# Stores moved to GpSimd's DMA queue in a WKV recurrence kernel

## The chip, the cores and the metric

The kernel runs on one core of one Trainium2 chip. The metric is device time in microseconds (us) of one execution, the median of several; the profile is of one execution and shows a span that is a little shorter than the timed one. The engines of the core are PE (TensorE, matmuls), DVE (VectorE), ACT (ScalarE), POOL (GpSimd) and SP (SyncE, which here only issues DMAs). DMAs can be issued by SP, ACT and POOL.

## The reference

For each of 16 batches and 256 channels a recurrence runs over 2048 time steps. It keeps a weighted sum `aa` of values and a sum `bb` of weights, with a running maximum `pp` so that no exponential overflows:

```python
for t in range(seq_len):
    ww = u + k[b, t]
    qq = np.maximum(pp, ww)
    e1, e2 = np.exp(pp - qq), np.exp(ww - qq)
    output[b, t] = (e1 * aa + e2 * v[b, t]) / (e1 * bb + e2 + 1e-08)
    ww = pp - w + k[b, t]
    qq = np.maximum(ww, k[b, t])
    e1, e2 = np.exp(ww - qq), np.exp(k[b, t] - qq)
    aa, bb, pp = e1 * aa + e2 * v[b, t], e1 * bb + e2, qq
```

k, v and the output are float32 arrays of 16 x 2048 x 256, 33.55 MB each, so 67.1 MB are read and 33.55 MB written.

## The kernel before

The kernel cuts time into 16 chunks of 128 steps, and each chunk into 4 groups of four batches. One such piece of k, v or the output is 128 x 1024 float32 values, 0.524 MB, and is called a pair; there are 64 of them, n = 4c + p for chunk c. The main loop has one slot for each pair. In slot n the exponentials of pair n are made (`exps`), k of pair n+2 is rounded for the matmuls (`round_k`), v of pair n+1 is cast to bfloat16 (`cast_v`), and the output of pair n-11 is finished: `den` and `recip` of pair q = n-10 make the reciprocals of its denominators in a buffer `rd`, and `num` and `mult` of pair qp = n-11 multiply the numerators in. Between them, spread over some slots, stand the steps that carry the state from chunk to chunk (`state_...`, `turn`, `inject`); `inject` writes the state into the ring EZR with four small DMAs, before `den` of the chunk's first pair reads it.

All large transfers go through SP's queue, in program order; only some loads of v, which convert to bfloat16 as they go, and the small transfers of `inject` are issued by GpSimd:

```python
    kpool = ctx.enter_context(tc.tile_pool(name="kpool", bufs=AHEAD))     # AHEAD = 6
    vpool = ctx.enter_context(tc.tile_pool(name="vpool", bufs=5))
    vbpool = ctx.enter_context(tc.tile_pool(name="vbpool", bufs=4))
    rpool = ctx.enter_context(tc.tile_pool(name="rpool", bufs=6))
# ... cut ...
    def v_mode(n):
        return "dma" if n >= LAG and n % 4 == 3 else "dve"                # LAG = 10
# ... cut ...
    def load_v(n, queue=SP):
        if v_mode(n) == "dma":
            VB[n] = vbpool.tile([128, 4, Dm], BF16, tag="vb", name="vb")
            K(POOL.dma_start(out=VB[n], in_=rows_of(v, n)))
        else:
            vr_of[n] = vpool.tile([128, 4, Dm], F32, tag="vr", name="vr")
            K(queue.dma_start(out=vr_of[n], in_=rows_of(v, n)))

    def load(n):
        for x, f in ((n - 1, load_v), (n, load_k)) if n < LAG + AHEAD else ((n, load_k), (n, load_v)):
            if x < NP and (f == load_k or v_mode(x) != "dma"):
                f(x)
# ... cut ...
    def state_next(c):
        # ... the state of the next chunk, two small operations on POOL ...
        if 4 * c + 11 < NP:
            load_v(4 * c + 11)
# ... cut ...
    def store(n):
        K(SP.dma_start(out=rows_of(out, n), in_=RD.pop(n).rearrange("p i (n d) -> p (i n) d", n=2)))
```

The main loop from slot 10 on, with the state steps (`small_work`) left in:

```python
    for n in range(LAG, NP):
        q, qp = n - LAG, n - LAG - 1
        load(n + AHEAD)
        if qp >= 0:
            num(qp, NUMB, 0)
        den(q)
        small_work(n, "nums")
        exps(n)
        small_work(n, "act")
        if qp >= 0:
            mult(qp, NUMB, 0)
        small_work(n, "mid")
        if n + 2 < NP:
            round_k(n + 2)
        if n + 1 < NP:
            cast_v(n + 1)
        # ... cut ...
        if qp >= 0:
            num(qp, NUMB, 1)
        sums(n - 1)
        recip(q, lambda: small_work(n, "recip"))
        if qp >= 0:
            mult(qp, NUMB, 1)
        small_work(n, "scan")
        if qp >= 0:
            store(qp)
        if n + 1 < NP:
            times_v(n)
            small_work(n, "chain")
            logs(n + 1)
        # ... cut ...
```

After the last slot eleven more rounds finish the outputs that are still open.

Of the kernel before, what the change touches and what calls it, by code (L numbers as in the profile page):

```python
# [11 lines left out]
ACT = mybir.ActivationFunctionType  # L12
# [3 lines left out]
def kernel(  # L16
# [9 lines left out]
    K = tc.keep_in_program_order  # L26
    PE, DVE, SC, POOL, SP = nc.tensor, nc.vector, nc.scalar, nc.gpsimd, nc.sync
# [6 lines left out]
    NP = 4 * NST  # L34
    RING = 12
    AHEAD = 6
    LAG = 10
# [5 lines left out]
    kpool = ctx.enter_context(tc.tile_pool(name="kpool", bufs=AHEAD))  # L43
    vpool = ctx.enter_context(tc.tile_pool(name="vpool", bufs=5))
    vbpool = ctx.enter_context(tc.tile_pool(name="vbpool", bufs=4))
    rpool = ctx.enter_context(tc.tile_pool(name="rpool", bufs=6))
    small = ctx.enter_context(tc.tile_pool(name="small", bufs=2))
    tiny = ctx.enter_context(tc.tile_pool(name="tiny", bufs=1))
    ps = ctx.enter_context(tc.tile_pool(name="ps", bufs=1, space=bass.MemoryType.PSUM))
# [2 lines left out]
    kr_of, vr_of, VB = {}, {}, {}  # L52

    def v_mode(n):
        return "dma" if n >= LAG and n % 4 == 3 else "dve"

    def rows_of(x, n):
        c, p = divmod(n, 4)
        return x[4 * p:4 * p + 4, c * TC:(c + 1) * TC, :].rearrange("n t d -> t n d")

    def load_k(n, queue=SP):
        kr_of[n] = kpool.tile([128, 4, Dm], F32, tag="kr", name="kr")
        K(queue.dma_start(out=kr_of[n], in_=rows_of(k, n)))
# [8 lines that stand above are left out]


    def load(n):
        for x, f in ((n - 1, load_v), (n, load_k)) if n < LAG + AHEAD else ((n, load_k), (n, load_v)):
            if x < NP and (f == load_k or v_mode(x) != "dma"):
                f(x)

# [99 lines left out]
    def round_k(n):  # L180
        km = consts.tile([128, 4, Dm], F32R, tag=f"km{n % 2}", name="km") if n < 2 else KM[n - 2]
        K(DVE.tensor_copy(km, kr_of.pop(n)))  # L182
        KM[n] = km
# [21 lines left out]
    def exps(n):  # L205
        if n < TURNS:
            for q in range(2):
                K(SC.activation(ez(n)[:, q], half(n, q), ACT.Exp))  # L208
        else:
            K(SC.activation(ez(n)[:, 0:2], PS[:, 0:4, :].rearrange("p (q i) x -> p q i x", q=2), ACT.Exp))  # L210

    def cast_v(n):
        mode = v_mode(n)
        if mode == "dma":
            return
        vb = vbpool.tile([128, 4, Dm], BF16, tag="vb", name="vb")
        vr = vr_of.pop(n)
        if mode == "act":
            K(SC.activation(vb, vr, ACT.Copy))
        elif mode == "pool":  # L220
            K(POOL.tensor_copy(vb, vr))
        else:
            K(DVE.tensor_copy(vb, vr))  # L223
        VB[n] = vb

    def times_v(n):
        vb = VB.pop(n).rearrange("p (i n) d -> p i (n d)", i=2)
        K(DVE.tensor_mul(ez(n)[:, 2:4], ez(n)[:, 0:2], vb.unsqueeze(1).broadcast_to([128, 2, 2, D])))  # L228
# [16 lines left out]
    def sums(n):  # L245
        c, p = divmod(n, 4)
        t = MISC[:, 0:Dm]
        for o in range(2):
            x = 24 - 16 * o - 2 * p
            for j in range(4):  # L250
                q, i = divmod(j, 2)
                K(PE.matmul(t[32 * j:32 * j + 32, :], mats["OH"][:, x:x + 32],  # L252
                            ez(n)[:, 2 * q, i, Dm * o:Dm * o + Dm],
                            start=p == 0 and o == 0, stop=p == 3 and o == 1,
                            tile_position=(0, 32 * j), skip_group_check=True))
# [97 lines left out]
    RD = {}  # L353

    def den(n):
        for m, q in (("L", 0), ("Id", 1)):
            for i in range(2):
                K(PE.matmul(DENB[:, i, :], mats[m], ez(n)[:, q, i, :], start=q == 0, stop=q == 1,  # L358
                            skip_group_check=True))
# [9 lines left out]
    def num(n, bank, i):  # L369
        for m, q in (("LN", 2), ("IdN", 3)):  # L370
            K(PE.matmul(bank, mats[m], ez(n)[:, q, i, :], start=q == 2, stop=q == 3, skip_group_check=True))  # L371

    def mult(n, bank, i):
        rd = RD[n]
        K(DVE.tensor_mul(rd[:, i, :], bank, rd[:, i, :]))  # L375

    def store(n):
        K(SP.dma_start(out=rows_of(out, n), in_=RD.pop(n).rearrange("p i (n d) -> p (i n) d", n=2)))

    def last_outputs(n, H):  # L380
        c, p = divmod(n, 4)
# [7 lines left out]
    for c in range(NST):  # L389
        s = 4 * c + 3  # L390
        plan = [(s + 1, "act" if s + 1 < LAG else "recip", copy_sums), (s + 1, "pe", turn),
                (s + 2, "act", state_logs), (s + 2, "mid", state_frames), (s + 2, "scan", state_scan), (s + 2, "scan", state_offsets),
                (s + 3, "recip", state_weights), (s + 3, "chain", state_chain),
                (s + 4, "nums", turn_back), (s + 4, "mid", inject), (s + 4, "mid", state_next)]
        if c == 0:
            plan = [(s + 1, "act", copy_sums), (s + 1, "pe", turn), (s + 2, "act", state_logs),
                    (s + 2, "chain", state_frames), (s + 2, "chain", state_scan), (s + 2, "chain", state_offsets),
                    (s + 3, "act", state_weights), (s + 3, "chain", state_chain),
                    (s + 4, "logs", turn_back), (s + 4, "logs", inject), (s + 4, "round", state_next)]
        if c == 1:  # L400
            plan = [(s + 1, "act", copy_sums), (s + 1, "pe", turn), (s + 2, "act", state_logs),
                    (s + 2, "chain", state_frames), (s + 2, "chain", state_scan), (s + 2, "chain", state_offsets)] + plan[6:]
        if c == NST - 1:
            plan = [(s + 1, "copy", copy_sums), (s + 1, "turn", turn),
                    (s + 1, "post", state_logs), (s + 1, "mid", state_frames), (s + 1, "mid", state_scan), (s + 1, "mid", state_offsets),
                    (s + 2, "post", state_weights), (s + 2, "first", state_chain),
                    (s + 3, "turn", turn_back), (s + 3, "first", inject)]
        for slot, where, f in plan:
            later.setdefault((slot, where), []).append((f, c))

    def small_work(n, where):
        for f, c in later.pop((n, where), []):
            f(c)
# [10 lines left out]
    logs(0)  # L424
    round_k(1)
    cast_v(0)
    for n in range(LAG):

# [19 lines left out]
    for n in range(LAG, NP):  # L448

        q, qp = n - LAG, n - LAG - 1  # L450
        load(n + AHEAD)
        if qp >= 0:
            num(qp, NUMB, 0)
        den(q)
# [17 lines that stand above are left out]
        if qp >= 0:  # L472
            mult(qp, NUMB, 1)
        small_work(n, "scan")
        if qp >= 0:
            store(qp)
        if n + 1 < NP:
            times_v(n)
            small_work(n, "chain")
            logs(n + 1)  # L480
        else:
            den(q + 1)
        small_work(n, "pe")
    sums(NP - 1)
    small_work(NP, "copy")
    late = []
    for n in range(NP, NP + LAG + 1):

        q, qp = n - LAG, n - LAG - 1
        H = PS[:, 2 * (n % 2):2 * (n % 2) + 2, :]  # L490
        for i in range(2):
            num(qp, H[:, i, :], i)
        small_work(n, "turn")
        if q < NP:
            recip(q, lambda: small_work(n, "recip"))
        small_work(n, "post")
        if q + 1 < NP:
            den(q + 1)
        small_work(n, "first")
        if qp == NP - 1:  # L500
            last_outputs(qp, H)
            break
        late.append((qp, H))
        if n != NP + 1:

            for x, bank in late:
                mult(x, bank, slice(0, 2))
                store(x)
            late = []
        small_work(n, "mid")  # L510
    assert not later
# [30 lines left out]
```

## Time and profile before

Three runs took 293.43, 293.82 and 293.94 us; the median is 293.82. The profiled execution has a span of 291.6 us.

| engine | busy us | share of the span |
|---|---|---|
| PE | 258.8 | 89% |
| DVE | 256.4 | 88% |
| ACT | 256.6 | 88% |
| POOL | 120.4 | 41% |

The DMA issues by line, with the size of one and the median time from issue to landing in us:

```profile
kr<-in_k_dram SPq DMA_DIRECT2D x64, 512.0 KB, 9.0
out_dram<-rd SPq DMA_DIRECT2D x63, 512.0 KB, 8.3
vr<-in_v_dram SPq DMA_DIRECT2D x50, 512.0 KB, 9.1
vb<-in_v_dram POOLq DMA_DIRECT2D x14, 256.0 KB, 8.5
EZR<-cb POOLq DMA_DIRECT2D x64, 8.0 KB, 5.2
```

How to read such lines: `out<-in` names the tiles or tensors, `SPq` the queue of the engine that issues, x64 the number of issues. A converting load (`vb`) is counted with the bytes that it writes, half of those that it reads. In a row of busy tenths the span is cut into 40 equal slices and each digit is the busy share of one slice, 9 for 90% and more. In a table of stages a row has the stretch in us, its length, then the busy time and number of instructions of PE, PE's weight loads, DVE, ACT and POOL, the granted clock of PE, the mean busy share of the 16 DMA engines (over 1 where requests overlap) and GB/s. In a list of waits a row says which engine waited at which line for what: us in total, times, the longest.

### The profile page before, as it was taken

What the parts mean: (1) busy time and instruction counts of PE and PEld (TensorE: products, weight loads), DVE (VectorE), ACT (ScalarE), POOL (GpSimd) and SP (SyncE); (2) the same over time, 40 slices, a digit from 0 to 9 for tenths busy, and PEclk for the clock granted to TensorE, in tenths of its full rate; (3) what the DMA queues carried; (4) which work ended last, traced back from release to release, by engine and by line L of the source; (5) the groups of instructions that cost most, each with busy time, mean ns of one, the idle gap of its engine ahead of it and who ended that gap; (6) DMA issues with size and microseconds to landing.
All of it is one profiled execution on the core that took longest, in us unless ns stands there. A gap on an engine that the chain in (4) does not pass through costs nothing. (4 is left out here: it accounts for less than half of the span.)

```text
span 291.6 us, 4937 instructions
## 1 busy us (share of the span) xinstructions
PE 258.8 (89%) x1662; PEld 120.1 (41%) x1694; DVE 256.4 (88%) x439; ACT 256.6 (88%) x253; POOL 120.4 (41%) x226
## 2 busy tenths in 40 slices
PE   5996998999999999988998999898899989988881
PEld 1433443444443444434443444444344444434330
DVE  4798899999999999999989989897998989886753
ACT  2586589999999999999899999989899998999892
POOL 7000345453544465553534555452455545342200
PEclk9699799999999999999999999999999999999997
DMA  7999999999999999999999999999999999984686
GB/s 228 351 348 349 347 323 329 297 385 332 374 351 360 375 338 382 338 371 336 380 342 370 377 336 378 331 385 334 373 380 336 381 333 382 334 283 153 220 288 216
DMA packets 103521, 97.86 MB, mean 336 GB/s; under 512 B 4156, under 2 KB 103496, under 8 KB 103496
## 3 DMA queue, kind: packets, MB, share of 16 engines
q1 hardware_dynamic: 93752, 93.08, 94.7%
q0 software_dynamic: 9440, 4.20, 10.0%
q10 hardware_dynamic: 304, 0.27, 0.3%
q8 instruction: 13, 0.21, 0.3%
q14 instruction: 12, 0.10, 0.1%
HBM read 67.12 MB, written 33.55 MB: 345 GB/s over the span
## 5 line engine op out<-in xcount | busy, mean ns | idle before, releaser
L210 ACT ACTIVATE EZR<-PS 128x2048 bf16<-128x2048 f32 x54 | 101.3, 1875 | 5.7 <-PE PS L197 4.9
L375 DVE TENSOR_TENSOR rd<-PS,rd 128x512 f32<-128x512 f32 (+1 forms) x118 | 85.9, 730 | 7.8 <-PE PS L371 6.6
L228 DVE TENSOR_TENSOR EZR<-EZR,vb 128x2048 bf16<-128x2048 bf16 x64 | 77.7, 1215 | 2.6 <-ACT EZR L208 1.5
L366 ACT ACTIVATE rd<-rd 128x1024 f32<-128x1024 f32 (+1 forms) x65 | 68.0, 1047 | 1.2
L364 ACT ACTIVATE rd<-PS 128x1024 f32<-128x1024 f32 (+1 forms) x65 | 65.9, 1013 | 1.7 <-PE PS L358 1.6
L348 POOL DMA_DIRECT2D EZR<-cb x64 | 38.2, 602 | 60.8 <-DVE cb L343 49.1
L371 PE MATMUL PS<-EZR,LN 128*128 128x512 bf16 x128 | 48.7, 380 | 13.7 <-DVE rd L375 10.3
L182 DVE CAST km<-kr 128x1024 fp32r<-128x1024 f32 x64 | 45.8, 715 | 11.9 <-DMA kr<-in_k_dram 11.8
L197 PE MATMUL PS<-km,NLE 128*128 128x512 f32 x128 | 47.8, 455 | 2.4 <-DVE km L182 2.4
L371 PE MATMUL PS<-EZR,IdN 128*128 128x512 bf16 x114 | 43.1, 378 | 0.0
L197 PE MATMUL PS<-km,NLZ 128*128 128x512 f32 x128 | 41.4, 406 | 0.0
L358 PE MATMUL PS<-EZR,L 128*128 128x512 bf16 x127 | 37.8, 379 | 1.7 <-ACT rd L364 1.7
L223 DVE CAST vb<-vr 128x1024 bf16<-128x1024 f32 x50 | 35.9, 719 | 0.8 <-DMA vr<-in_v_dram 0.8
L358 PE MATMUL PS<-EZR,Id 128*128 128x512 bf16 x114 | 35.0, 379 | 0.1
L283 POOL TENSOR_TENSOR F<-LL,LL 128x32 f32<-128x32 f32 x13 | 7.9, 604 | 51.1 <-ACT LL L274 51.1
L191 PE MATMUL PS<-WU,CO 32*128 32x512 bf16 x256 | 26.7, 391 | 2.2 <-DVE WU L423 1.7
L208 ACT ACTIVATE EZR<-PS 128x1024 bf16<-128x1024 f32 x20 | 19.4, 1020 | 10.2 <-PE PS L197 10.2
L252 PE MATMUL PS<-EZR,OH 128*32 128x256 bf16 x512 | 26.1, 280 | 2.1
L197 PEld LDWEIGHTS PS<-km,NLZ 128*128 128x128 f32 x128 | 24.7, 193 | 5.8
L197 PEld LDWEIGHTS PS<-km,NLE 128*128 128x128 f32 x128 | 19.4, 191 | 17.4 <-issue 13.8
L371 PEld LDWEIGHTS <-IdN 128*128 128x128 bf16 x128 | 12.5, 97 | 26.7 <-issue 23.9
L296 POOL TENSOR_TENSOR Q<-P,F 128x64 f32<-128x64 f32 x13 | 15.7, 1204 | 12.1 <-DVE P L287 12.1
(72 smaller groups left out, 213.7 us busy)
## 6 DMA issues: line engine op xcount, KB each, us to landing
kr<-in_k_dram SPq DMA_DIRECT2D x64, 512.0 KB, 9.0
out_dram<-rd SPq DMA_DIRECT2D x63, 512.0 KB, 8.3
vr<-in_v_dram SPq DMA_DIRECT2D x50, 512.0 KB, 9.1
vb<-in_v_dram POOLq DMA_DIRECT2D x14, 256.0 KB, 8.5
EZR<-cb POOLq DMA_DIRECT2D x64, 8.0 KB, 5.2
out_dram<-rd SPq DMA_DIRECT2D x2, 128.0 KB, 3.0
out_dram<-rd ACTq DMA_DIRECT2D x2, 128.0 KB, 3.3
wuf<-in_w_dram ACTq DMA_DIRECT2D x1, 8.0 KB
```

The costliest lines, as they stand in the source:

```text
L182: K(DVE.tensor_copy(km, kr_of.pop(n)))
L191: K(PE.matmul(half(n, q)[:, i, :], CO[g:g + 32, :], WU[g:g + 32, :].unsqueeze(1).broadcast_to([32, 2, Dm]), start=True, stop=False, tile_p ...
L197: K(PE.matmul(half(n, q)[:, i, :], (NLE, NLZ)[q], km[:, i, :], start=False, stop=True, skip_group_check=True))
L210: K(SC.activation(ez(n)[:, 0:2], PS[:, 0:4, :].rearrange("p (q i) x -> p q i x", q=2), ACT.Exp))
L223: K(DVE.tensor_copy(vb, vr))
L228: K(DVE.tensor_mul(ez(n)[:, 2:4], ez(n)[:, 0:2], vb.unsqueeze(1).broadcast_to([128, 2, 2, D])))
L348: K(POOL.dma_start(out=EZR[r:r + 1, 2 * q, r0:r0 + 4, :, :].rearrange("o p i (b x) -> o (p i b) x", b=4), in_=cb[x:x + 32, :]))
L358: K(PE.matmul(DENB[:, i, :], mats[m], ez(n)[:, q, i, :], start=q == 0, stop=q == 1, skip_group_check=True))
L364: K(SC.activation(rd[:, i, :], DENB[:, i, :], ACT.Ln, scale=RS))
L366: K(SC.activation(rd[:, i, :], rd[:, i, :], ACT.Exp, scale=-1.0))
L371: K(PE.matmul(bank, mats[m], ez(n)[:, q, i, :], start=q == 2, stop=q == 3, skip_group_check=True))
L375: K(DVE.tensor_mul(rd[:, i, :], bank, rd[:, i, :]))
```

## The change

Stores of the main loop are issued by GpSimd instead of SP, two slots after the slot in which their data is made, so that SP's queue carries only loads; `rd` has eight buffers instead of six to allow for it. The outputs finished after the main loop are still stored by SP. Loads of v that convert as they go begin with pair 15 instead of 11. The state steps of the first chunk stand one slot sooner. The order in `load` is written in one form for all slots, and unused ways of casting v are taken out.

```diff
-    rpool = ctx.enter_context(tc.tile_pool(name="rpool", bufs=6))
+    rpool = ctx.enter_context(tc.tile_pool(name="rpool", bufs=8))
...
     def v_mode(n):
-        return "dma" if n >= LAG and n % 4 == 3 else "dve"
+        return "dma" if n > 11 and n % 4 == 3 else "dve"
...
     def load(n):
-        for x, f in ((n - 1, load_v), (n, load_k)) if n < LAG + AHEAD else ((n, load_k), (n, load_v)):
-            if x < NP and (f == load_k or v_mode(x) != "dma"):
-                f(x)
+        if n - 1 < NP and v_mode(n - 1) != "dma":
+            load_v(n - 1)
+        if n < NP:
+            load_k(n)
...
-    def store(n):
-        K(SP.dma_start(out=rows_of(out, n), in_=RD.pop(n).rearrange("p i (n d) -> p (i n) d", n=2)))
+    def store(n, queue=POOL):
+        K(queue.dma_start(out=rows_of(out, n), in_=RD.pop(n).rearrange("p i (n d) -> p (i n) d", n=2)))
...
         if c == 0:
-            plan = [(s + 1, "act", copy_sums), (s + 1, "pe", turn), (s + 2, "act", state_logs),
-                    (s + 2, "chain", state_frames), (s + 2, "chain", state_scan), (s + 2, "chain", state_offsets),
-                    (s + 3, "act", state_weights), (s + 3, "chain", state_chain),
-                    (s + 4, "logs", turn_back), (s + 4, "logs", inject), (s + 4, "round", state_next)]
+            plan = [(s + 1, "act", copy_sums), (s + 1, "pe", turn), (s + 1, "pe", state_logs),
+                    (s + 1, "chain", state_frames), (s + 1, "chain", state_scan), (s + 1, "chain", state_offsets),
+                    (s + 2, "act", state_weights), (s + 2, "chain", state_chain),
+                    (s + 3, "logs", turn_back), (s + 3, "logs", inject), (s + 3, "round", state_next)]
... (main loop, slot n, qp = n - 11)
         load(n + AHEAD)
+        if qp >= 2:
+            store(qp - 2)
...
         small_work(n, "scan")
-        if qp >= 0:
-            store(qp)
... (after the main loop)
+    store(NP - LAG - 3)
+    store(NP - LAG - 2)
...
                 mult(x, bank, slice(0, 2))
-                store(x)
+                store(x, SP)
```

In the plan `s` is 4c + 3, so for the first chunk `inject` and `state_next` move from slot 7 to slot 6. The line in `state_next` that loads v of pair 4c + 11 is not touched.

More of the change, by code (lines that the diff above doesn't have):

```diff
@@ L212, in cast_v @@
     def cast_v(n):
-        mode = v_mode(n)
-        if mode == "dma":
+        if v_mode(n) == "dma":
             return
@@ L217, in cast_v @@
         vr = vr_of.pop(n)
[L218 to L223, printed above, removed]
+        K(DVE.tensor_copy(vb, vr))
         VB[n] = vb
```

## The prediction

> **What bounds the kernel now.** I read four views in this order: the page's busy shares and its row of DMA shares, the table of stages, the waits, and the timeline of SyncE's queue.
>
> ```profile
> PE 258.8 (89%) x1662; PEld 120.1 (41%) x1694; DVE 256.4 (88%) x439; ACT 256.6 (88%) x253; POOL 120.4 (41%) x226
> DMA  7999999999999999999999999999999999984686
> ```
>
> Three engines stand at 88 to 89%, so the shares name no bound; the DMA engines are at 9 tenths in all but the last slices. The stages say more:
>
> ```profile
> 46.00:112.00 66.00, 63.17 (x427) 29.98 (x436) 64.26 (x105) 64.75 (x63) 34.48 (x60) 1.00 1.12 353
> 112.00:252.00 140.00, 127.49 (x849) 60.37 (x864) 128.69 (x207) 131.38 (x125) 65.86 (x116) 1.00 1.11 360
> 252.00:291.60 39.60, 29.21 (x160) 12.52 (x162) 26.09 (x43) 32.01 (x35) 8.56 (x17) 0.96 0.74 236
> ```
>
> The columns are PE, PEld, DVE, ACT, POOL, clock, DMA share, GB/s. From 46 to 112 us ACT is busy 98%: the exps, logarithms and reciprocals set the pace. From 112 to 252 ACT is down to 94%. The waits say what on:
>
> ```profile
> DVE km L182 <- DMA kr<-in_k_dram: 11.8, 27, 1.2
> ACT EZR L210 <- PE PS L197: 4.9, 10, 1.4
> SPq L378 <- ACT EZR L210: 16.9, 17, 1.7
> ```
>
> 11.0 of the 11.8 us that VectorE waits for k lie between 112 and 253 us. The beat of POOL's update at line 327 gives the size: it starts at 65.01, 80.82, 96.64, 112.42 (15.8 us for four slots, 3.95 each), but at 145.97, 162.73, 179.53, 196.35 (16.8, or 4.2 each). So the first half runs at ScalarE's pace and eats the lead of the loads; the second runs at the pace of the DMA.
>
> Is the DMA really full, or does SyncE hold loads back when it waits for a store's data (third line)? Five more stretches:
>
> ```profile
> 22.00:36.00 14.00, 11.27 (x80) 5.13 (x80) 11.98 (x23) 8.59 (x11) 2.58 (x6) 0.88 1.09 348
> 44.00:46.00 2.00, 1.26 (x9) 0.53 (x8) 1.93 (x7) 2.00 (x3) 0.00 (x0) 1.00 1.27 265
> 125.00:129.00 4.00, 3.60 (x27) 1.72 (x28) 3.93 (x7) 3.60 (x4) 2.61 (x5) 1.00 1.09 383
> 134.00:137.00 3.00, 2.75 (x20) 1.27 (x20) 2.49 (x5) 2.87 (x5) 1.01 (x3) 1.00 1.23 279
> 138.00:143.00 5.00, 4.22 (x30) 1.82 (x29) 4.65 (x10) 4.33 (x6) 1.77 (x5) 1.00 1.09 384
> ```
>
> Loads alone run at 348 GB/s, two loads to a store at 383 to 384, without a dip. The low rows are where a converting load runs; it is counted with the 0.262 MB it writes, not the 0.524 MB it reads. 134 to 137 us: 279 x 3 = 0.84 MB counted, 1.10 MB of source, 366 GB/s. Check over four slots: 12 transfers of 0.524 MB are 6.29 MB; 1.10 MB take the 3 us, the other 5.19 MB take 13.5 us at 384; 16.5 us, and the beat is 16.8. The queue is never empty, and SyncE's waits cost nothing: the requests already in the ring (9 us from issue to landing) cover them.
>
> ```profile
> 244.34 1.74 SPq L63 DMA_DIRECT2D kr<-in_k_dram  x1
> 246.20 40.20 SPq L378 DMA_DIRECT2D out_dram<-rd  x17
> ```
>
> The last k is issued at 244.34, and its rounding starts at 252.7, the start the page of k's tile gives for the last one. Ahead of it in the queue stand 46 stores (counted in the timeline). What follows 252.7 is 39 us of computing that the DMA does not limit (chain of waits: PE, ACT and DVE). So the time is: bytes moved before the last k has landed, over the rate, plus 39 us.
>
> **What the Trainium skill says.** "DMA: Bandwidth & Descriptors", section "Issuing engines are not separate DMA queues": DMAs from SyncE, ScalarE and GpSimd run on the same 16 DMA engines and interleave; another issuer saves only issue time. The trace agrees: from 134 to 137 us the total stays at 366. Same page, "Queues, rings and completion order": each DMA engine takes turns between its rings, packet by packet. From 44 to 46 us, beside loads alone, the counted 265 GB/s are what equal numbers of 1 KB and 0.5 KB packets give at 353 GB/s of source, against 348 for loads alone: equal shares, nothing gained or lost. "SBUF — State Buffer", section "Who interferes with whom": VectorE's two-port casts and GpSimd lock each other out, also when it writes descriptors. Here a converting load holds GpSimd 0.89 us on average, with VectorE at 92%, so the lock is bearable.
>
> **The change part by part.**
>
> 1. Stores 0 to 52 go to GpSimd. Its cost: 53 x 0.89 us (the converting load has as many rows) = 47 us, so POOL goes from 120 to about 167 us busy, 57%. It waits 3 to 4 us before its small steps in each chunk, so this is beside the path. A store issued in slot n has data from slot n-2 and never waits in earnest. Eight buffers for rd: the tile is wanted again five slots (20 us) after its store is issued; nothing waits there. SyncE keeps only loads, which will now be stopped by buffers, not by stores.
>
> 2. Bytes are the same, and so is the rate: GpSimd's ring and SyncE's take turns. What changes is who is served first. Before, 46 stores preceded the last k. After, stores leave when their data is there: when k of pair 63 is due in slot 61, store 48 has been issued, and those from about two slots back (5 us of start-up as for the small EZR transfers, 2.7 us of moving at half the rate) have landed: 47 to 48. That is 1.5 more, 1.5 x 0.524 MB / 384 GB/s = 2.0 us later.
>
> 3. Stretches in which loads run alone. Per slot a store at half of 384 GB/s takes 2.7 us, converting load and small transfers about 0.9 us per slot; in the other 0.6 us of a 4.2 us slot loads run alone, at 348 and not 384: 0.6 x 36/384 = 0.056 us, over the 50 slots from 11 to 61 2.8 us. The 16 DMA engines drift apart, as the steady 384 before shows (there too loads come in pairs), so I count half: 1.4 us.
>
> 4. Converting loads from pair 15 on. Pair 11 now goes through SyncE, in load(12). But state_next(0) still asks for load_v(11), and as that pair is no longer converting it loads v of 11 a second time: 51 needed + 1 loads, 0.524 MB more, in a phase where loads run at 348: 1.5 us. I take 0.7 off, as SyncE waits there now and then for a free buffer. One more cast on VectorE (0.72 us) lies in slot 10, where the engines are not yet at their pace.
>
> 5. The first state step one slot sooner: same instructions. Before, PE waits only 0.2 us for the first EZR transfer. It makes room for transfers that now stand behind stores; of itself it brings nothing in a phase that is paced by loads.
>
> 6. The rewritten load(): the order on SyncE's queue stays v(n-1), k(n). Nothing.
>
> Sum: 2.0 + 1.4 + 1.5 - 0.7 = +4.2 us: 293.8 + 4.2 = 298.
>
> **Rivals.**
>
> - SyncE freed: if the waits of SyncE had cost rate, or if two rings moved more than one, the 1.0 us per four slots would vanish, ScalarE would bound throughout, about 9 us less: 285. For it: 17 waits of SyncE on lines that produce a store's data, and loads that may run six slots ahead instead of four. Against it: 384 GB/s without a dip during those waits, and 366 with two rings.
> - Two rings lose: if load against store costs what 366 against 384 shows (5%) while both rings are full, some 3.6 of each 4.2 us, 50 slots pay 0.17 us each, 8.6 us in place of the 1.4: 305. I read the 366 as the greater share of reads (0.83, between 384 at two thirds and 348 at all), which halves the stores' part of it.
> - The state's rows late: the EZR transfers now queue behind a store in one ring. They are issued by 128.5, needed by the den matmuls at 137.1, and land after 5.2 us: 3 to 4 us to spare. One store ahead takes 2.7 of them; two would make PE wait over 1 us per chunk, 13 chunks: beyond 305.
>
> **Range and chances.** The lever that the change pulls on is, as I read it, not the bound; every effect I can size is a small loss. The 8 in 10 range runs from 292.5 (the losses absent, a little order gained) to 304.5 (the second rival). 2% is 5.9 us: faster means under 287.9, which needs the first rival, 0.07; slower means over 299.7, 0.35; within, 0.58.
>
> **What would show it.** The page should read 67.65 MB from HBM instead of 67.12, 52 loads of v by SyncE and 13 by POOL. VectorE's wait for k should stay or grow (11 to 16 us), with a beat near 16.9 us per four slots in the second half and not 15.8; the last k's rounding should start near 257. The stages with both rings should show the same 370 to 384 GB/s at a DMA share of about 1.2. POOL near 167 us. I am wrong if the wait for k vanishes and the beat falls to 15.8, or if PE waits for EZR in each chunk.

## The result, and the profile after

The changed kernel takes 300.28 us (median of 4 runs, 300.19 to 300.38) against 293.62 us before (293.39 to 293.94): a ratio of 1.0226 with a 95% interval of 1.0208 to 1.0244. The loss of 6.7 us lies within the range and is 2.3 us larger than the 4.4 us that the predicted 298.0 makes against these 293.62. It lies above the 299.7 that the prediction called slower and gave 0.35, not in the band that it gave 0.58. The span of the profiled execution is 298.6 us, 7.0 more.

First the page of the changed kernel: busy shares, the row of DMA shares, the packets and the two large DMA queues, and the bytes.

```profile
PE 267.2 (89%) x1694; PEld 120.7 (40%) x1694; DVE 258.4 (87%) x440; ACT 257.7 (86%) x253; POOL 154.5 (52%) x278
...
DMA  6999999999999999999999999999999999935786
...
DMA packets 83698, 98.65 MB, mean 330 GB/s; under 512 B 4172, under 2 KB 76888, under 8 KB 83672
...
q1 hardware_dynamic: 66824, 66.33, 69.0%
q0 software_dynamic: 16544, 31.73, 33.1%
...
HBM read 67.65 MB, written 33.55 MB: 339 GB/s over the span
```

The same part of the page of the kernel before, which the prediction didn't show:

```profile
DMA packets 103521, 97.86 MB, mean 336 GB/s; under 512 B 4156, under 2 KB 103496, under 8 KB 103496
...
q1 hardware_dynamic: 93752, 93.08, 94.7%
q0 software_dynamic: 9440, 4.20, 10.0%
```

q0 is GpSimd's queue, q1 SyncE's. The shares of the engines and the row of nines tell as little as they did before. What is new stands in the packet counts. Before, no packet lay between 2 and 8 KB. After, 83672 - 76888 = 6784 are between 2 and 8 KB, and 6784 = 53 x 128: a store by GpSimd, 0.524 MB, moves in 128 packets of 4 KB, where SyncE moves a store of the same size in 512 packets of 1 KB. The prediction read none of these lines.

The table of stages after, with the columns of before (PE, PEld, DVE, ACT, POOL, clock, DMA share, GB/s):

```profile
46.00:112.00 66.00, 64.22 (x414) 29.72 (x415) 61.86 (x102) 60.79 (x60) 43.76 (x71) 0.95 1.11 348
112.00:252.00 140.00, 127.71 (x854) 58.08 (x852) 127.62 (x206) 129.92 (x123) 84.78 (x145) 1.00 1.10 356
252.00:260.00 8.00, 6.95 (x43) 3.50 (x40) 6.91 (x10) 7.57 (x8) 5.25 (x11) 1.00 1.03 304
260.00:298.60 38.60, 29.00 (x162) 12.35 (x160) 25.34 (x42) 30.63 (x33) 10.25 (x19) 0.96 0.65 217
```

From 46 to 112 us the queues give 348 GB/s instead of 353 and from 112 to 252 us 356 instead of 360, and ACT is down from 98% to 92% in the first of these. The last row is the tail after the last k.

The waits after, then those of SyncE's own queue:

```profile
DVE km L183 <- DMA kr<-in_k_dram: 12.5, 16, 1.5
...
ACT EZR L211 <- PE PS L198: 10.1, 11, 4.3
```

```profile
SPq L63 <- DVE EZR L223: 36.8, 9, 5.1
...
SPq L71 <- DVE rd L370: 21.5, 15, 4.3
...
SPq L71 <- DVE EZR L223: 18.9, 9, 3.6
```

VectorE still waits for k. SyncE, which now issues only loads in the main loop, waits on VectorE's lines, that is for VectorE to free the buffers of k and v; its nine longest rows of this kind sum to 136 us. So the loads are always asked for as early as the buffers allow, and still come late. The 4.3 us of ScalarE are one stop at slot 12 (47 to 51.5 us); two kernels below have the same start and end at 293.7 and 294.1, so it is hidden behind the DMA.

The DMA issues after, with the median time from issue to landing at the end of each row:

```profile
kr<-in_k_dram SPq DMA_DIRECT2D x64, 512.0 KB, 12.5
out_dram<-rd POOLq DMA_DIRECT2D x53, 512.0 KB, 8.3
vr<-in_v_dram SPq DMA_DIRECT2D x52, 512.0 KB, 12.2
...
vb<-in_v_dram POOLq DMA_DIRECT2D x13, 256.0 KB, 8.5
EZR<-cb POOLq DMA_DIRECT2D x64, 8.0 KB, 5.7
```

A load of k needs 12.5 us instead of 9.0. Last, the end of SyncE's loads in the timeline, and the row of the rounding of k (duration min, median, max; first and last start):

```profile
240.90 5.51 SPq L63 DMA_DIRECT2D kr<-in_k_dram  x1
246.50 1.00 SPq L71 DMA_DIRECT2D vr<-in_v_dram  x1
247.55 2.07 SPq L63 DMA_DIRECT2D kr<-in_k_dram  x1
```

```profile
L183 DVE CAST km<-kr x64: 678/686/969, 4.9 to 259.6; 128x1024 fp32r<-128x1024 f32 x64
```

The last k is issued 3.2 us later than before and rounded at 259.6 instead of 252.7. Those 6.9 us are the whole loss of the span; the tail has kept its length.

**Two terms.** The prediction's form, bytes moved before the last k over the rate, can be filled in from the records of single packets. This is my count over each trace (a converting load at its source bytes). "Bytes" is the difference in MB to the kernel before, divided by its 365.4 GB/s; "rate" is what remains of the later start. The kernels below the second row are the experiments of the next section.

```
              last k    MB moved   mean     bytes   rate
              rounded   by then    GB/s     us      us
before        252.7     92.36      365.4
after         259.6     93.67      360.8    +3.6    +3.3
a_once        257.0     92.71      360.8    +1.0    +3.3
b_pool        257.1     92.99      361.8    +1.7    +2.7
a_sp          253.1     91.88      363.0    -1.3    +1.7
b_step        253.7     92.36      364.0     0.0    +1.0
b_lag2        250.6     91.29      364.3    -2.9    +0.8
s_lag2        251.8     91.39      363.0    -2.7    +1.8
q_early       258.7     93.77      362.5    +3.9    +2.1
```

The small EZR transfers are counted at twice their bytes in every row, 0.5 MB too much, so the means are 2 GB/s high and the differences stand. The last column is not the work of GpSimd's queue alone: the kernels whose stores all stay with SyncE (a_sp, b_step, b_lag2, s_lag2) have 0.8 to 1.8 us there.

### The profile page after: what moved, and what is told of

Its sections match the earlier page's. It is cut to its first block, busy times and chain, and to the rows that moved or that the text cites. A ratio compares the mean times of both kernels' runs of the same rounds, so it can differ in the third digit from the quotient of the medians.

```text
span 298.6 us, 4995 instructions
## 1 busy us (share of the span) xinstructions
PE 267.2 (89%) x1694; PEld 120.7 (40%) x1694; DVE 258.4 (87%) x440; ACT 257.7 (86%) x253; POOL 154.5 (52%) x278
## 2 busy tenths in 40 slices
DMA packets 83698, 98.65 MB, mean 330 GB/s; under 512 B 4172, under 2 KB 76888, under 8 KB 83672
## 5 line engine op out<-in xcount | busy, mean ns | idle before, releaser
L223 DVE TENSOR_TENSOR EZR<-EZR,vb 128x2048 bf16<-128x2048 bf16 x64 | 78.6, 1229 | 2.3 <-ACT EZR L209 1.7
L343 POOL DMA_DIRECT2D EZR<-cb x64 | 38.6, 609 | 39.5 <-DVE cb L338 34.4
L183 DVE CAST km<-kr 128x1024 fp32r<-128x1024 f32 x64 | 45.5, 712 | 12.7 <-DMA kr<-in_k_dram 12.5
L198 PE MATMUL PS<-km,NLE 128*128 128x512 f32 x128 | 48.5, 461 | 0.8 <-DVE km L183 0.8
L366 PE MATMUL PS<-EZR,IdN 128*128 128x512 bf16 x128 | 48.9, 382 | 0.0
L373 POOL DMA_DIRECT2D out_dram<-rd x53 | 42.3, 802 | 1.8 <-DVE EZR L223 1.8
L353 PE MATMUL PS<-EZR,L 128*128 128x512 bf16 x128 | 38.5, 383 | 1.8 <-ACT rd L359 1.8
L218 DVE CAST vb<-vr 128x1024 bf16<-128x1024 f32 x51 | 37.4, 733 | 1.4 <-DMA vr<-in_v_dram 1.4
L353 PE MATMUL PS<-EZR,Id 128*128 128x512 bf16 x128 | 38.2, 380 | 0.0
L366 PEld LDWEIGHTS <-IdN 128*128 128x128 bf16 x128 | 12.5, 98 | 31.3 <-issue 28.8
## 6 DMA issues: line engine op xcount, KB each, us to landing
kr<-in_k_dram SPq DMA_DIRECT2D x64, 512.0 KB, 12.5
```

What stands on the lines that cost most here:

```text
L198: K(PE.matmul(half(n, q)[:, i, :], (NLE, NLZ)[q], km[:, i, :], start=False, stop=True, skip_group_check=True))
L343: K(POOL.dma_start(out=EZR[r:r + 1, 2 * q, r0:r0 + 4, :, :].rearrange("o p i (b x) -> o (p i b) x", b=4), in_=cb[x:x + 32, :]))
L373: K(queue.dma_start(out=rows_of(out, n), in_=RD.pop(n).rearrange("p i (n d) -> p (i n) d", n=2)))
```

## The experiments

**1. The second load taken out (a_once).** From the changed kernel:

```diff
-        if 4 * c + 11 < NP:
+        if 4 * c + 11 < NP and v_mode(4 * c + 11) == "dma":
             load_v(4 * c + 11)
```

> After, with v of pair 11 loaded once. Theory (bytes ahead of the last k, over the mean rate): 0.524 MB less at about 0.37 MB per us is 1.4 us, so 298.9 us; 67.12 MB read. Rival (the loss is the 4.3 us stop of ScalarE at 47 to 51 us, which begins with the wait for the second load of v 11): the stop goes away and the time falls by 3 to 4 us, to about 297. Rival (GpSimd's descriptor writing slows VectorE and the state steps): no change, 300.3.

Measured: 298.61 us, ratio 1.0157 (1.0140 to 1.0173) to the kernel before. The second load of pair 11 costs 1.7 us (300.28 to 298.61; 1.9 if each is taken beside its own runs of the kernel before). It costs about what it moves: 0.524 MB at 360.8 GB/s are 1.5 us. The rest of the loss, 4.7 us against the 293.88 of the kernel before beside it, is still there.

**2. The same stores by SyncE (a_sp).** From the changed kernel, one word; the second load stays:

```diff
-    def store(n, queue=POOL):
+    def store(n, queue=SP):
```

> After, with all stores issued by SyncE, still two slots behind; second load of v 11 kept. Theory: the rate goes back to about 376 GB/s of source bytes (-3.3 us), and as SyncE's queue is one line again, two stores fewer than before the change stand ahead of the last k, 44 in place of 47.4 (3.4 x 1.4 = -4.7 us): about 292.3 us, below before in spite of the second load. Rival (only the queue's way matters, not who is served first): -3.3 us, 297. Rival (the stop at 47 to 51 us is the loss): stays at 300.

Measured: 293.71 us, ratio 0.9998 (0.9990 to 1.0007). The issuer of the stores is worth 6.6 us. Everything else of the change, the delay of two slots, the buffers, the second load, the plan, is in this kernel, and it is no slower than the one before. The table above splits the 6.5 us by which its last k comes sooner: 1.79 MB fewer ahead of it, 4.9 us, and 1.6 us for the rate. So the issuer acts mostly through the order, as GpSimd's queue lets stores pass that SyncE's queue holds back behind loads. The expected 292.3 was missed by 1.4 us: the rate did not come back to that of the kernel before (363.0 against 365.4), for which experiments 4 and 6 give reasons. Its stages:

```profile
46.00:112.00 66.00, 63.11 (x414) 29.35 (x415) 62.90 (x104) 60.48 (x60) 30.85 (x56) 0.97 1.12 351
112.00:252.00 140.00, 133.40 (x891) 61.98 (x890) 131.62 (x214) 134.54 (x128) 66.59 (x119) 1.00 1.11 358
```

**3. Only the stores by GpSimd (b_pool).** From the kernel before: `rd` with eight buffers, stores two slots late by GpSimd, those after the main loop by SyncE. Nothing else of the change:

```diff
-    rpool = ctx.enter_context(tc.tile_pool(name="rpool", bufs=6))
+    rpool = ctx.enter_context(tc.tile_pool(name="rpool", bufs=8))
...
-        K(SP.dma_start(out=rows_of(out, n), ...
+        K(queue.dma_start(out=rows_of(out, n), ...      # queue=POOL
...
+        if qp >= 2:
+            store(qp - 2)
...
-        if qp >= 0:
-            store(qp)
...
-                store(x)
+                store(x, SP)
```

> Before, with nothing but the stores changed: by GpSimd, two slots behind, eight buffers. Theory: all of the loss but the second load's 1.4 us comes with the stores: 298.9 us, second-half beat 17.2 us per four slots. Rival (state step and converting loads carry the loss): 293.6.

Measured: 298.19 us, ratio 1.0137 (1.0117 to 1.0157), with 293.88 for the kernel before beside it: 4.3 us for the move of the stores alone. Its stages, and the last start of the rounding:

```profile
46.00:112.00 66.00, 63.87 (x431) 29.42 (x431) 63.44 (x104) 64.48 (x63) 44.13 (x72) 1.00 1.11 350
112.00:250.00 138.00, 125.41 (x833) 57.18 (x833) 124.80 (x201) 127.69 (x121) 84.09 (x145) 1.00 1.10 356
```

```profile
L182 DVE CAST km<-kr x64: 679/688/989, 4.8 to 257.1; 128x1024 fp32r<-128x1024 f32 x64
```

ScalarE keeps its 98% from 46 to 112 us, and the second stage loses the same 4 GB/s (356 for 360). The count splits the 4.4 us at the last k into 1.7 for 0.63 MB more moved ahead of it and 2.7 for the rate.

**4. Only the earlier state step and the later converting loads (b_step).** From the kernel before: the plan of chunk 0 as in the change, `v_mode` with `n > 11`, and v of pair 11 loaded once.

```diff
-        return "dma" if n >= LAG and n % 4 == 3 else "dve"
+        return "dma" if n > 11 and n % 4 == 3 else "dve"
...
-        if 4 * c + 11 < NP:
+        if 4 * c + 11 < NP and v_mode(4 * c + 11) == "dma":
... (the plan of chunk 0, as in the change)
```

> Before, with only the first state step one slot sooner and converting loads from pair 15 on (v of 11 loaded once). Theory: same bytes ahead of the last k, so the time of before, 293.9 +- 0.4, even if ScalarE again stops for some us at slot 12. Rival (that stop is part of the loss): 3 us slower, 297.

Measured: 294.06 us, ratio 1.0015 (1.0007 to 1.0023), beside 293.67: 0.4 us slower. The parts add up: 4.3 (stores) + 0.4 (plan and converting loads) + 1.7 (second load) = 6.4 of 6.7 us.

**5. Rows of rd set apart (p_pad).** If the 4 KB packets came from rows that lie beside each other in SBUF, 32 bytes between rows of 1 KB should break them up. From a_once:

```diff
-            rd = rpool.tile([128, 2, D], F32, tag="rd", name="rd")
+            rd = rpool.tile([128, 2, 2, Dm + 8], F32, tag="rd", name="rd")[:, :, :, 0:Dm]
... (the uses of rd take the four rows apart)
```

> After, v of pair 11 loaded once, and rd padded by 8 values behind each row of 256, so that a store's rows of 1 KB stand apart in SBUF and GpSimd's queue moves them in 1 KB packets as SyncE's does. Theory: the rate fell because a store's 4 KB packets take four fifths of the DMA engines' turns, and loads are then left alone at 348 GB/s; with equal packets the turns are equal, the stretches of loads alone shorten, and the mean rate rises from 370 towards 376: 298.6 - 1.5 to 2.5 = 296 to 297 us. Rival (stores issued by GpSimd cost rate whatever their packets): stays at 298.6 or is slower, as there are four times the packets.

Measured: 298.89 us, ratio 1.0176 (1.0163 to 1.0190), as a_once; the expected 296 to 297 did not come. But the packets didn't change, so the run can't decide what it was made for:

```profile
q0 software_dynamic: 16544, 31.73, 33.3%
```

That is the row of the padded kernel: the packets and bytes of a_once to the last digit. The stores by GpSimd move in 4 KB packets with the rows 32 bytes apart too. So no experiment shows that the packet size is the cause of the lower rate; what speaks for it is below, from the packets.

**What the packets show.** In the changed kernel, packets of the two queues begun in each of some 1 us stretches (my count; in brackets the mean time of one):

```
us         GpSimd's queue         SyncE's queue
64 to 65   -                      340 x 1 KB (51 ns)
65 to 66   -                      339 x 1 KB (51 ns)
77 to 78   79 x 4 KB (159 ns)      84 x 1 KB (48 ns)
78 to 79   78 x 4 KB (159 ns)      93 x 1 KB (46 ns)
79 to 80   81 x 4 KB (159 ns)      78 x 1 KB (46 ns)
81 to 82   -                      364 x 1 KB (48 ns)
```

While these stores run (two, one behind the other), the queues take turns packet by packet, about 80 of each in a us; the store gets 80 x 4096 B = 328 GB/s and the loads 80 x 1024 B = 82 GB/s. The stretches of the changed kernel with loads alone and with a store, then the latter stretch of the kernel before, where loads and stores share one ring:

```profile
63.00:67.00 4.00, 3.89 (x29) 1.70 (x28) 3.93 (x10) 3.97 (x5) 3.46 (x4) 1.00 1.09 348
77.00:80.00 3.00, 2.94 (x23) 1.25 (x21) 2.92 (x6) 3.00 (x5) 2.86 (x6) 1.00 1.05 413
```

```profile
77.00:80.00 3.00, 2.74 (x23) 1.27 (x22) 3.00 (x7) 2.97 (x3) 1.68 (x3) 1.00 1.09 384
```

At 328 GB/s a store would pass in 0.524 MB / 328 GB/s = 1.6 us. That is the clean case. From 112 us to the last k of the changed kernel, where the loads set the pace, the median store takes 2.8 us from its first packet to its last. By the packets in steps of 0.05 us, these 147.6 us hold:

```
                                         us     GB/s
a store under way, no 512 B packets      71.3   386 (208 of them the store's)
a store, and packets of 512 B            25.2   375
no store, but packets of 512 B           20.8   347
loads alone, in packets of 1 KB          30.2   343
```

The packets of 512 B are those of converting loads and EZR transfers. Where there are none the mean is 373 GB/s; in the kernel before, counted in the same way from 112 us to its last k, it is 380. In whole us without them, half of those before lie between 379 and 385 GB/s, half of those after between 364 and 399. So the ring that holds both kinds gives a steady mix, and GpSimd's stores make a rich mix that alternates with stretches of loads alone and is on the mean a little slower: 370 GB/s from 112 us to the last k with everything counted, against 376. This alternation is measured. That the 4 KB packets are its reason, and not the second queue, is not shown, though q_loads and q_early of experiment 7, with the large packets on the loads, reach 382 and 383 GB/s from two queues.

**6. The order alone: stores by SyncE, but later (s_lag2, b_lag2, b_lag4).** If the time is set by what stands ahead of the last k, then a store issued later in the same ring should gain. s_lag2 is the changed kernel with its stores by SyncE and v of pair 11 loaded once; b_lag2 is the kernel before with eight buffers and this edit; b_lag4 has 4 in place of 2:

```diff
         load(n + AHEAD)
+        if qp >= 2:
+            store(qp - 2)
...
-        if qp >= 0:
-            store(qp)
... (after the main loop)
+    store(NP - LAG - 3)
+    store(NP - LAG - 2)
```

> After, stores by SyncE two slots behind and v of pair 11 loaded once. Theory: before has 46 stores ahead of the last k, this one 44, nothing else differs in bytes: 293.6 - 2 x 1.4 = 290.9 us. Rival (who is served first doesn't matter, the whole traffic does): 293.6.

> Before, with stores still by SyncE but two slots later and eight buffers; state steps and converting loads as before. Theory: two stores fewer ahead of the last k; the two runs with late SyncE stores gave about 1.0 us for each store, so 293.9 - 1.9 = 292.0. Rival (the state step one slot sooner is what made the late-store run faster than before): 293.9.

> The same with stores four slots later, still eight buffers. Theory: four stores fewer, 293.9 - 4 x 1.0 = 290. Rival (buffers of rd come free too late, as a store now has only three slots, 12 us, to be issued and landed before its buffer is wanted): ScalarE waits, and the time is above that of the two-slot version.

Measured: s_lag2 291.98 us, ratio 0.9937 (0.9923 to 0.9950); b_lag2 291.61 us, 0.9941 (0.9920 to 0.9963); b_lag4 294.96 us, 1.0040 (1.0027 to 1.0052). Two slots bring 44 stores ahead of the last k instead of 46, 1.07 MB less by the count, and the last k is rounded 2.1 us sooner:

```profile
L182 DVE CAST km<-kr x64: 679/686/864, 5.1 to 250.6; 128x1024 fp32r<-128x1024 f32 x64
```

That is 1.0 us for each store put off, of the 1.4 us that its bytes take at the mean rate. An estimate from the measured rates explains the difference: a store with the two loads of its slot, 1.573 MB, takes 4.10 us at 384 GB/s, the two loads alone take 3.01 us at 348, so the store adds 1.1 us. This is also about what b_lag2 has in the last column of the table of terms, 0.8 us for two stores. s_lag2 and b_lag2 are both faster than the kernels before and after, and nothing in this study is faster; which of the two is the better one their intervals don't tell. Each also differs from a kernel above in nothing but the issuer of the main loop's stores: a_once to s_lag2 is 6.6 us, b_pool to b_lag2 6.6 us by the medians and 5.8 by the ratios, as in experiment 2. With four slots the rival took over; VectorE's wait for k is down to 0.3 us, but ScalarE waits for a buffer that a store still holds, a row that the kernel before doesn't have:

```profile
ACT rd L364 <- DMA out_dram<-rd: 9.6, 16, 1.4
```

**7. The packets turned round: loads by GpSimd, stores by SyncE (q_loads, q_k, q_early, q_earlyP).** If turns by packet favour the ring with 4 KB packets, then the loads, which the time hangs on, should have it. q_loads is b_lag2 with the loads of the main loop by GpSimd from slot 10 on and the EZR transfers by SyncE from the second chunk on; q_k moves k alone:

```diff
             if x < NP and (f == load_k or v_mode(x) != "dma"):
-                f(x)
+                f(x, POOL if n >= LAG + AHEAD else SP)
...
-                K(POOL.dma_start(
+                K((POOL if c < 1 else SP).dma_start(
                     out=EZR...
```

> The turned-round split, on the version with SyncE's stores two slots late (291.6 us): from slot 10 on all loads of k and v are issued by GpSimd, stores stay with SyncE, and the small EZR transfers go with the stores from the second chunk on. Theory (GpSimd's transfers move in 4 KB packets and take about four fifths of the turns beside 1 KB packets; what is ahead of the last k decides): now loads are served first and stores wait, the wait of VectorE for k goes away, the beat stays at 15.8 us per four slots throughout, and the time falls to about 286 us. Rival (two rings as such cost rate, or loads alone cannot pass 348 GB/s): 291 to 294. Rival (GpSimd's descriptor writing and its waits hold up the state steps): above 294, with ScalarE waiting for POOL.

> The same with only the loads of k (and the converting ones) by GpSimd; other loads of v stay with SyncE ahead of the stores. Theory: k is served first, but v and stores share one ring and v comes late instead: between 286 and 291.6 us. Rival (GpSimd's load of work decides): halfway between 291.6 and what the run with all loads shows, whichever side that is.

Measured: q_loads 300.53 us, ratio 1.0216 (1.0180 to 1.0253); q_k 301.24 us, 1.0246 (1.0226 to 1.0266). Both are slower, and neither theory came true; q_k is not between 291.6 us and q_loads either. Yet the steady part of q_loads does what it should. Two stages and two rows of waits of q_loads:

```profile
46.00:70.00 24.00, 16.49 (x93) 6.94 (x92) 13.08 (x19) 13.29 (x14) 7.77 (x13) 0.79 0.89 284
...
112.00:259.00 147.00, 138.95 (x933) 64.05 (x932) 139.35 (x225) 141.67 (x136) 94.19 (x146) 1.00 1.09 365
```

```profile
DVE km L182 <- DMA kr<-in_k_dram: 10.6, 4, 6.0
...
PE PS L358 <- DMA EZR<-cb: 4.5, 3, 3.2
```

From 112 us on the rate is 365 on this row (382 by source bytes in the count of the packets, against 376 before; q_k has 368), k lands 7 to 13 us before it is used, and the beat of POOL's update at line 327 is 16.0 us up to 168 us. But some 10 us are lost when the queue is changed (slot 16 begins at 74.6 us, in b_lag2 at 64.2): a k that SyncE had issued at 38.2 us landed only at 55.6. From 46 to 52 us GpSimd's loads, issued later and needed later, moved in 409 packets of 4 KB beside 441 of 1 KB from SyncE: equal turns, and four fifths of the bytes. Another 3 us go at slot 42, where the small EZR transfers stand in SyncE's ring behind a starved store.

q_early avoids the change in mid-loop: GpSimd takes every load of the main loop from slot 0 on, SyncE only the first six k and five v, and all EZR transfers. q_earlyP is the same with the EZR transfers left to GpSimd.

```diff
-                f(x)
+                f(x, POOL if n >= 6 else SP)
...
-                K(POOL.dma_start(
+                K(SP.dma_start(                     # q_early; q_earlyP keeps POOL
                     out=EZR...
```

> Stores by SyncE two slots late, and all loads from slot 0 on by GpSimd, the small EZR transfers by SyncE; only the first six k and five v go by SyncE. What the two kernels with the loads moved at slot 10 lost was the change of queue: loads left in SyncE's ring were starved by those that GpSimd issued after them. If so, nothing is left behind here, exps of slot 13 starts near 56 us and not at 63, and the 378 GB/s that the loads gave in the second half count in full: last k's rounding near 246, about 287 us. The EZR transfers behind starved stores may still cost some 3 us near slot 42: 290. Rival: the pace of a store starved by loads is what limits (its buffers come free late, ScalarE waits for rd), or GpSimd's issue of 117 loads is itself too slow: then 295 or more whatever the start.

> As the other of this call, but the EZR transfers stay with GpSimd, behind loads instead of behind stores. If starved stores made EZR late, TensorE's wait for EZR goes away and this is the faster of the two, near 287 us. If a ring full of loads makes the EZR transfers late (up to six loads ahead of one, some 8 us, against 8 us of time to spare), TensorE waits for EZR in many chunks and it is slower than the other, above 295.

Measured: q_early 299.56 us, ratio 1.0204 (1.0169 to 1.0240); q_earlyP 307.02 us, 1.0419 (1.0388 to 1.0449). The expectation of 287 to 290 was a miss: the loss at the change of queue only moved to the start. Two rows of waits of q_early between 18 and 34 us, and its stage from 22 to 32 us:

```profile
POOL vr L71 <- DVE LN L161: 10.4, 1, 10.4
...
DVE vb L223 <- DMA vr<-in_v_dram: 6.2, 1, 6.2
```

```profile
22.00:32.00 10.00, 4.53 (x27) 2.05 (x27) 5.02 (x9) 2.45 (x4) 2.61 (x4) 0.52 0.91 284
```

From 22 to 24 us the packets stand at 133 of 4 KB to 146 of 1 KB: the last v that SyncE had issued (at 12.1 us) got its 75 GB/s beside GpSimd's loads and landed some 18 us after issue. VectorE waited for it, so no buffer of v came free, and GpSimd stood with its next load 10.4 us long. Slot 13 began at 61.2 us (52.2 in b_lag2). After that q_early runs at 4.00 us per slot from 12 to 38, and TensorE waits 4.3 us in three places for late EZR transfers, as in q_loads. In q_earlyP TensorE waits for EZR once, 1.3 us, so that rival fell, and that its time is above 295 as the rival said is luck; it is slower for a reason that wasn't foreseen. GpSimd waits in order for load buffers, and its small state steps behind them come late: VectorE and ScalarE wait 11.0 and 11.1 us for them, at lines 287 and 304. A load ring of GpSimd without a loss at its start was not found.

## Why the prediction was right in direction and 2.3 us short

- **The bound.** Right. The tail after the last k is 38.7 to 39.5 us in every kernel above, and the times follow the moment of its rounding.
- **Rival 1, SyncE freed.** Fell. SyncE has 136 us of waiting for buffers, so loads are issued as early as can be, and VectorE's wait for k is 12.5 us, not gone. The beat grew from 16.8 to about 17.2 us (133.2 to 253.8 us in seven beats), where I named 16.9.
- **Step 2, stores first (2.0 us).** About right: 0.63 MB in b_pool, 1.7 us.
- **Step 3, loads alone (1.4 us).** The kind of loss was right and the size was not: b_pool gives 2.7 us in its place (the 3.3 of a_once also hold the plan and the converting loads, 1.0 in b_step). "Half of 384 GB/s" for a store, 2.7 us, holds on the average of the second half (2.8 us, 208 of 386 GB/s) but not where the packets of both queues alternate, 328 of 413. What failed is "The 16 DMA engines drift apart, so I count half": loads alone ran for 30.2 of the 147.6 us, 0.9 us of each slot where the term had 0.6 and then halved its cost. The equal shares of the prediction came from 44 to 46 us, beside a converting load: 335 packets of 0.5 KB and 335 of 1 KB, a measurement of another kind of transfer on that queue. The Trainium skill had the rule in what I cited, "DMA: Bandwidth & Descriptors", section "Queues, rings and completion order", turns packet by packet; and the section "SWDGE vs HWDGE vs iDMA" of the same page says, of the path that GpSimd's DMAs take, that a packet has preferably at most 4096 bytes. Turns count packets, not bytes, as the counts above show. That GpSimd's plain copies fill theirs and SyncE's don't is read from the packet rows of the two pages.
- **Step 4, the second load (1.5 - 0.7 us).** The 1.5 was about right (1.7 to 1.9 measured), the deduction was wrong: a queue that is full from first to last has no free time to give.
- **Step 5, the earlier state step (0).** With the converting loads 0.4 us, measured in b_step.
- **Rival 2, two rings lose (305).** Too large, and not for its reason: I read 366 beside a converting load as its mark. Beside a store two rings carry more, 413 at best and 386 on the mean; what is lost is lost between the stores. The sign that both rings would show 370 to 384 GB/s did not come true in this form.
- **Rival 3, EZR late.** Fell for this change: landing went from 5.2 to 5.7 us, and TensorE doesn't wait for it in each chunk. It came true only where a starved store stood ahead (q_loads, q_early).
- **POOL.** 154.5 us busy, not 167: a store holds GpSimd 0.80 us, not 0.89, so 53 are 42.3 us, and the other work on GpSimd shows some 8 us less than before (its spans are rough).

With 2.7 in place of 1.4, 1.7 in place of 0.8, 1.7 for 2.0 and 0.4 for 0 the sum is 6.5 us, of 6.7 measured. Still open: whether the packet size as such, or any burst of stores from a second queue, makes the lower rate. It would take GpSimd's stores in 1 KB packets, which the padding didn't bring.

## What to carry to other kernels

Before a stream is moved to another queue, look at the packet sizes on the page: queues took turns by packet here, so where 4 KB packets stood against 1 KB the bytes went 4 to 1, and the one starved should not be the one that the time hangs on. In a kernel that is bound by DMA with a tail of computing, count what stands ahead of the last load: the larger part of what the issuer of the stores was worth here is that order, not the rate. A store put off behind the last load, at no cost but two buffers, gained 1.0 us. Such a delay ends where its buffers run out, and a change of queue costs the transfers that are still in the old one.

## What the runs showed of the hardware that was not expected

- Plain copies of 1 KB rows issued by GpSimd moved in 4 KB packets (159 ns each beside loads), those by SyncE in 1 KB packets (46 to 51 ns); 32 bytes between the rows in SBUF changed nothing.
- The rate depends on the mix: 348 GB/s for loads alone, 384 for two loads to a store in one ring, 413 while a 4 KB store runs against 1 KB loads. Loads against loads in packets of 4 and 1 KB (q_early, 22 to 24 us) gave 347, so in these runs it is reads beside writes that gain, not large packets.
- An instruction that issues a load on GpSimd waits in order with its arithmetic; in q_earlyP this cost other engines 22 us of waiting.
